# Hybrid decoder step on one core: page cache laid out for contiguous compression, keys and values multiplied page by page, more conditioning weights loaded ahead

## The chip, the core and the metric

The kernel runs on one core of a Trainium2 chip. The metric is device time of one launch in microseconds (us). TensorE (PE) multiplies, VectorE (DVE), ScalarE (ACT) and GpSimd (POOL) do the elementwise work, SyncE (SP), POOL and ACT issue transfers. Tensors lie on 128 partitions; a row of the profile such as `128x256` gives partitions by elements.

## The reference, cut to what matters

The layer is a hybrid decoder for 512 prompt tokens and 8 sample tokens of width 1024. The change touches its beginning (the conditioning, the first norm) and the compressed branch of the attention:

```python
mod = jnp.einsum("bd,de->be", jax.nn.silu(c), p["ada_w"]) + p["ada_b"]
sh1, sc1, g1, sh2, sc2, g2 = jnp.split(mod[:, None, :], 6, axis=-1)
h = _rmsnorm(x, p["norm1_w"]) * (1.0 + sc1) + sh1
proj = h @ p["w_in"]
...
def _compress(k, pe, w1, w2):          # k: (b, length, 4 heads, 64); 16 rows make a block
    sub = k[:, :nj * CMP_STRIDE].reshape(b, nj, CMP_STRIDE, N_KV_HEADS, ATT_HEAD_DIM)
    hid = jnp.einsum("ld,lde->e", pe, w1)
    for r in range(nsub):              # nsub = 2: each window is two blocks
        part = jnp.einsum("bjshd,sde->bjhe", sub, w1[r * CMP_STRIDE:(r + 1) * CMP_STRIDE])
        hid = hid + part[:, r:r + nc]
    return jnp.einsum("bnhe,ed->bnhd", jax.nn.silu(hid), w2)
...
past = cache_nsa_kv[page_table]        # 16 pages of 128 rows: k_cmp, v_cmp, k_sel, v_sel
```

For the samples `_compress` runs on the cached keys and values of 16 pages, for the prompt on those just projected. Behind it come a state-space scan, the attention, an output projection and a feed-forward block.

## The kernel before

All activations stand transposed: features on partitions, tokens in the free dimension. A dense product of one 128-wide output tile is 8 steps over k; each step is three products (high by high, high by low, low by high; the weights and the activations are split into two float32r parts) of the two halves of the tokens, six matmuls. `Weights` loads tiles ahead into a few raw buffers and splits them by half tiles: the high part on ACT (L302), the low part in turn on DVE and POOL (L304). `mm` (L379) issues nearly every matmul, `act` (L424), `tt` (L408), `stt` (L411) and `ts` (L416) nearly all elementwise work, so that groups of the profile go by tile names.

The program goes in stages; a planner lets a side stream (scan, attention) run between the steps of the main stream (dense products) at a ratio taken from an earlier pass, and a scheduler orders each engine's instructions.

- **Phase A** (`phase_a`, L644), the first 107 us. SP loads `w1k`, the first matrix of the key compression (`w`), and a few small arrays. POOL, in order, gathers the 16 pages of cached keys and values to be compressed (tiles `S` and `KS`, eight pages each; each gather is a transfer that POOL has to describe), loads the activations `xT` between them in four parts, then `w1v` and six tiles of conditioning weights (`ada`). All further loads of this phase are issued by SP as buffers come free. PE multiplies the pages by the compression matrices (`compress_s`, L1138: keys first, in groups of four pages, then values, in groups of eight, in 72 + 5 per step slices between other work). The norm follows: squares and their running sum `S` (ACT, DVE), the sums over features (`s<-ones,S`), their reciprocal root in five columns (`rstd5`), spread over the partitions by matmuls with the identity (`<-cst,rstdb`), copied into `rs`. Then four steps: two blocks of 256 conditioning columns (`ada`, L571: eight matmuls, a copy `adas`, two transposes, a reduction and an addition into `mod`), and `h(k)` (L692) for two of the eight feature blocks: x times rs, the scaling `a`, the high part on ACT, scale and shift on DVE, the low part on DVE. The dense products of the first two tiles (`misc` and `B`) take a block as it comes.
- **The scan**, to about 515 us: the rest of the input projection for the state-space branch, with the scan beside it.
- **The attention**, to about 1000 us. It begins with `cmp_tile` (L1073): the rotated keys and values of a head are copied by pairs of rows into `KP` (tile `K`, L1111), two copies on ACT and two on DVE for each of four heads. `compress_p` (L1162) multiplies `KP` by the same compression matrices, 32 matmuls of 132 columns, beside the dense products of the first head. `setup_c` puts the position table into `KP` by eight small transfers.
- Output projection and feed-forward to the end.

A float32 matmul leaves two records in the profile (and two rows of the counts there), a float32r one leaves one. The loops the steps turn on are these: the moving operand of the compression reads one element in eight.

```python
self.mm(o[:, x:x + n], w1[:, j, half, i, :], KS[x // 8][:, x % 8:x % 8 + n, j, :, i:64:8], ...)   # L1149
self.mm(pp, w[:, i * P:(i + 1) * P], self.KP[:, j, :, pr:pr + 257:8], ...)                         # L1173
```

Of the kernel before, what the change touches and what calls it, by code (L numbers as in the profile page):

```python
# [37 lines left out]
def _in_proj_tiles():  # L38
    """Column lists of w_in, one per 128-wide tile, in the order of use (-1 is a zero column)."""
# [66 lines left out]
NC0 = 72  # L106
NC1 = 5
# [29 lines left out]
def layout(a):  # L137
    """Inputs of kernel() -> arrays of the launch: layout only, and constants of the shapes."""
# [26 lines left out]
    r["pek"] = np.ascontiguousarray(a["cmp_pe_k"].reshape(16, P).T)  # L165
    r["pev"] = np.ascontiguousarray(a["cmp_pe_v"].reshape(16, P).T)
    cache = a["cache_nsa_kv"]
    ks = cache[:, :, 0:2].reshape(NPAGE, 64, 2, 2, N_KV, 64)
    r["pool_cmp"] = np.ascontiguousarray(ks.transpose(0, 2, 5, 3, 4, 1)).reshape(NPAGE * P, 512)
# [49 lines left out]
def unlayout(o):  # L219
    """Arrays of the launch -> the reference's outputs: layout only."""  # L220
# [22 lines left out]
class Weights:  # L243
    """Operand tiles in their order of use: loaded ahead, and split, half a tile at a time, into two float32r parts that
    add up to them.

    Without an order (the first of two passes) it takes them as they are asked for, and notes the order."""
# [3 lines left out]
    def __init__(self, nc, pool, jobs, order, raws=2, parts=5, queue=None):  # L251
        """queue(i): the function that issues load number i."""
        self.queue = queue
# [22 lines left out]
    def load(self):  # L276
        while self.loaded < len(self.order) and len(self.raw) < self.raws:
            i = self.loaded
            src, nk, _ = self.jobs[self.order[i]]
            pool, n = self.place(("r", i), [("r", j) for j in self.raw], self.more and self.more[1])  # L280
# [5 lines left out]
    def prepare(self):  # L286
        """Split the next half tile, if there is room for its parts."""
# [26 lines left out]
    def get(self, key):  # L314
        """The next tile: itself if it is not split, else its number for half()."""
# [17 lines left out]
    def half(self, i, x):  # L333
        """The parts of half x of tile number i."""
# [3 lines left out]
    def drop_half(self, i, x):  # L338
        """These parts are no longer read."""
# [4 lines left out]
    def drop(self, key):  # L344
        """A tile that is not split is no longer read."""
# [5 lines left out]
class Aside(float):  # L351
    """A cost in a mix of streams, but none of the stream's."""


class Emit:
# [29 lines left out]
    def after_side(self, r):  # L385
        """Keep a matmul of the main stream from running far ahead of the side stream."""
# [4 lines left out]
    def queue(self, out, src):  # L391
        """A load behind the one queued before it."""
# [7 lines left out]
    def behind(self, r, last):  # L400
        """Issue r behind the instruction last of the same engine."""
# [242 lines left out]
    def phase_a(self):  # L644
        nc, A, cp = self.nc, self.A, self.cp
        with self.tc.tile_pool(name="pa", bufs=1, reuse_waits="tile") as pa:
# [28 lines left out]
            def some(n):  # L675
                for _ in range(n):
                    next(comp, None)
# [1251 lines left out]
```

## Time and profile before

| | |
|---|---|
| time, three runs | 1514.46 us median (1514.32 to 1515.28) |
| span of the profiled execution | 1514.7 us |
| PE busy | 1450.5 us (96%) |
| DVE, ACT, POOL busy | 944.1 (62%), 696.0 (46%), 471.9 (31%) us |
| moved | 195.34 MB, mean 129 GB/s |

The span goes from the first to the last instruction of one profiled execution and stands 0.2 us from the median of the unprofiled runs. In the rows below, a line begins with its start and its duration in us or, in the grouped views, with the line of the kernel; `xN` counts instructions, and a bracket tells how long the engine had been idle and what ended that. A PE duration contains the drain of the last matmul, so the pace of a stream is read from starts.

### The profile page before, as it was taken

The page shows a single profiled execution, that of the slowest core. Times are in us where ns is not written, and L with a number is a line of the kernel's source. Part 1 is how long each engine was busy: PE and PEld are TensorE (multiplying, and loading weights), DVE is VectorE, ACT ScalarE, POOL GpSimd, SP SyncE. Part 2 cuts the span into 40 slices and gives each one's busy share as a digit, 9 for nine tenths or more (in the row PEclk, how much of TensorE's full clock was granted, in tenths as well). Part 3 has the DMA queues.
Part 4 walks back from the last instruction along what each step waited for, and adds up shares of the span by engine and source line. Part 5 has one row for each costly group of instructions (what it writes and reads, how often), then busy time and mean ns, then how long its engine had stood idle before and what let it go on. Part 6 is the DMA issues. An engine that isn't in the chain of part 4 may idle for free.

```text
span 1514.7 us, 28764 instructions
## 1 busy us (share of the span) xinstructions
PE 1450.5 (96%) x11327; PEld 1302.7 (86%) x11327; DVE 944.1 (62%) x1851; ACT 696.0 (46%) x1538; POOL 471.9 (31%) x479
## 2 busy tenths in 40 slices
PE   6989899999999899999999999999989999999996
PEld 6569789998998889787878877779989999999996
DVE  1368899879788854866768562124476635653663
ACT  1246666565565324655546463213454423432443
POOL 6112454554473745212203011112431111111113
PEclk9999999999999999999999999999999999999998
DMA  8445545446345274313122124334522234423221
GB/s 289 155 157 156 175 149 171 154 133 202 112 154 177 92 256 165 128 55 117 64 85 78 50 98 148 118 97 178 196 76 93 84 98 140 139 98 100 89 75 57
DMA packets 74807, 195.34 MB, mean 129 GB/s; under 512 B 9488, under 2 KB 22320, under 8 KB 74416
## 3 DMA queue, kind: packets, MB, share of 16 engines
q1 hardware_dynamic: 69840, 178.25, 35.7%
q0 software_dynamic: 4288, 14.72, 2.8%
q8 instruction: 89, 1.46, 0.4%
q10 hardware_dynamic: 544, 0.54, 0.1%
q14 instruction: 46, 0.38, 0.1%
HBM read 173.15 MB, written 24.49 MB: 130 GB/s over the span
## 4 chain that ended last, share of the span: by engine, by line
PE 72%; DVE 8%; DMA 3%; POOL 3%; ACT 2%; issue 2%; SPq 0%; DVEq 0%; POOLq 0%; ACTq 0%
PE d L379 54%; PE s L379 14%; PE s L1342 2%; DVE st L411 1%; DVE S L408 1%; DMA wr<-w_in 1%; DVE wl L304 1%; POOL wl L304 1%; DVE so L408 1%; DVE E L408 1%; POOL sq L408 1%; DMA st<-sst 1%; ACT so L424 1%; POOL yd L408 1%; ACT E L424 0%
## 5 line engine op out<-in xcount | busy, mean ns | idle before, releaser
L379 PE MATMUL d<-S,wh 128*128 128x256 f32 (+1 forms) x4640 | 838.9, 291 | 27.1 <-DVE S L408 9.9
L379 PEld LDWEIGHTS d<-S,wh 128*128 128x128 f32 x4640 | 673.3, 191 | 61.1 <-issue 34.0
L379 PE MATMUL d<-S,wl 128*128 128x256 f32 (+1 forms) x2672 | 559.4, 287 | 0.0
L379 PEld LDWEIGHTS d<-S,wl 128*128 128x128 f32 x2672 | 423.3, 190 | 6.9 <-issue 6.3
L304 POOL TENSOR_TENSOR wl<-wr,wh 128x512 fp32r<-128x512 f32 (+1 forms) x153 | 210.2, 1375 | 664.4 <-ACT wh L302 607.7
L302 ACT ACTIVATE wh<-wr 128x512 fp32r<-128x512 f32 (+1 forms) x354 | 217.0, 623 | 401.5 <-PE d L379 319.8
L304 DVE TENSOR_TENSOR wl<-wr,wh 128x512 fp32r<-128x512 f32 (+1 forms) x201 | 154.2, 767 | 112.4 <-ACT wh L302 99.9
L379 PE MATMUL d<-M,wh 128*128 128x256 f32 (+1 forms) x960 | 197.3, 284 | 1.5 <-DVE M L411 0.8
L379 PEld LDWEIGHTS d<-M,wh 128*128 128x128 f32 x960 | 149.8, 188 | 2.1 <-DVE M L411 1.0
L424 ACT ACTIVATE P<-s,sm 128x256 f32<-128x256 f32 (+3 forms) x128 | 66.8, 525 | 64.6 <-DVE sm L1324 60.5
L408 DVE TENSOR_TENSOR S<-S,S 128x520 f32<-128x520 f32 (+3 forms) x86 | 65.1, 760 | 34.5 <-ACT S L424 32.0
L1324 DVE TENSOR_REDUCE sm<-s 128x1 f32<-128x512 f32 (+3 forms) x96 | 57.2, 596 | 31.5 <-PE s L379 30.6
L424 ACT ACTIVATE S<-S 128x520 f32<-128x520 f32 (+4 forms) x87 | 49.7, 579 | 52.5 <-DMA S<-xT 24.3
L411 DVE SCALAR_TENSOR_TENSOR S<-d,fww,S 128x511 f32<-128x511 f32 x84 | 62.9, 749 | 12.0 <-ACT S L424 12.0
L424 ACT ACTIVATE PT<-s 128x512 f32<-128x512 f32 (+2 forms) x96 | 49.9, 524 | 38.8 <-PE s L1342 38.5
L411 DVE SCALAR_TENSOR_TENSOR st<-st,dts,so 128x128 f32<-128x128 f32 x128 | 59.7, 516 | 11.3 <-ACT so L424 7.7
L379 PE MATMUL s<-PT,V 128*64 128x128 f32 x640 | 64.3, 286 | 0.0
L379 PE MATMUL s<-K,Q 128*128 128x256 f32 (+3 forms) x256 | 60.2, 337 | 1.7 <-ACT PT L424 1.6
L416 DVE TENSOR_SCALAR P<-P,sm,gates 128x256 f32<-128x256 f32 (+3 forms) x128 | 59.7, 487 | 2.4
L424 ACT ACTIVATE so<-bcb,xd 128x128 f32<-128x128 f32 x128 | 41.0, 391 | 38.1 <-DVE ys L1033 30.5
L411 DVE SCALAR_TENSOR_TENSOR S<-d,cwh,S 128x511 f32<-128x511 f32 (+2 forms) x72 | 53.3, 741 | 1.6 <-ACT S L424 1.2
L1342 PE MATMUL s<-cst,P 128*128 128x128 f32 x320 | 52.3, 275 | 0.9 <-DVE P L416 0.7
(304 smaller groups left out, 1744.5 us busy)
## 6 DMA issues: line engine op xcount, KB each, us to landing
wr<-w_in SPq DMA_DIRECT2D x77, 512.0 KB, 3.8
wr<-w_up SPq DMA_DIRECT2D x44, 512.0 KB, 3.7
wr<-ada SPq DMA_DIRECT2D x42, 512.0 KB, 3.8
st<-sst SPq DMA_DIRECT2D x32, 256.0 KB, 2.7
csb<-dr_cs SPq DMA_DIRECT2D x16, 512.0 KB, 3.7
o_ssms<-st SPq DMA_DIRECT2D x32, 256.0 KB, 3.0
wr<-w_so SPq DMA_DIRECT2D x16, 512.0 KB, 3.7
wr<-w_dn SPq DMA_DIRECT2D x16, 512.0 KB, 3.5
```

The lines of the kernel that those rows point to most:

```text
L302: self.nc.scalar.activation(hi[:, :n], raw[:, k0:k1], AF.Copy)
L304: eng.tensor_tensor(out=lo[:, :n], in0=raw[:, k0:k1], in1=hi[:, :n], op=ALU.subtract)
L379: r = self.nc.tensor.matmul(out, lhsT=l, rhs=r, start=start, stop=stop)
L408: return (eng or self.nc.vector).tensor_tensor(out=out, in0=a, in1=b, op=op)
L411: return self.nc.vector.scalar_tensor_tensor(out=out, in0=a, scalar=s, in1=b, op0=op0, op1=op1)
L416: return (eng or self.nc.vector).tensor_scalar(out=out, in0=a, scalar1=s1, scalar2=s2, op0=op0, op1=op1)
L424: return self.nc.scalar.activation(out, a, func, scale=scale, **kw)
L1324: nc.vector.tensor_reduce(sm[:, 0], ps, AX.X, ALU.max, negate=True)
L1342: nc.tensor.transpose(ps[:, i * n + k * P:i * n + (k + 1) * P], pr[:, i, k * P:(k + 1) * P], self.ident)
```

## The change

The cached pages are laid out on the host as (8, 8) row pairs with the block position i outside: the eight rows that one matmul reads now lie side by side. `compress_s` is one nest: for each group of four pages, keys and values, both halves, eight i, so 128 matmuls of 128 columns in all where there were 64 of 128 and 32 of 256. Its sums stand in the two double-bank tiles `d`. The prompt's `KP` has the same order, so `cmp_tile` writes it contiguously from a source that is read every 16th element, and the position table comes by one transfer and two POOL copies. SP loads `w1k` and `w1v` first; POOL gathers eight pages before the first part of x. The first eight `ada` tiles get buffers of their own (`first`, in two 16 KB tiles) besides the six raw ones, and all 14 are queued on POOL at once. Twelve bf16 matmuls of zeros stand at PE's start. The table for the square root is loaded early. The sums of the norm stand before the last group of pages, the spreading behind it in two halves, and x times rs stands ahead of the `h(k)` steps.

```diff
-    r["pool_cmp"] = np.ascontiguousarray(ks.transpose(0, 2, 5, 3, 4, 1)).reshape(NPAGE * P, 512)
+    ks = cache[:, :, 0:2].reshape(NPAGE, 8, 8, 2, 2, N_KV, 64)
+    r["pool_cmp"] = np.ascontiguousarray(ks.transpose(0, 3, 6, 4, 2, 5, 1)).reshape(NPAGE * P, 512)
...
+            self.warm(pa)
...
+            for j, nm in enumerate(("w1k", "w1v")):
+                for half in range(2):
+                    self.queue(w1[:, j, half], A[nm][half])
+                if j == 0:
+                    self.queue(cT, A["cT"])
...
-                if i % 4 == 3:
-                    k = i // 4 * 2
-                    self.queue_pool(x[:, k:k + 2], A["xT"][:, k:k + 2])
-            for half in range(2):
-                self.queue_pool(w1[:, 1, half], A["w1v"][half])
+                if i in (7, 11):
+                    load_x((i - 7) // 2)
+            load_x(4)
+            load_x(6)
+            first = [self.t(cp, "S16", [P, 4, 1024], 4) for _ in range(2)]
             W = Weights(nc, pa, self.jobs(), self.order and self.order[0], raws=RAW0, parts=PART0,
-                        queue=lambda i: self.queue_pool if i < RAW0 else self.queue)
+                        queue=lambda i: self.queue_pool if i < 8 + RAW0 else self.queue,
+                        first=[first[i // 4][:, i % 4] for i in range(8)])
...
+        for x in range(0, 16, 4):
+            for j in range(2):
+                for half in range(2):
+                    for i in range(8):
+                        self.mm(ps[j][:, half, x:x + 4], w1[:, j, half, i, :],
+                                KS[x // 8][:, x % 8:x % 8 + 4, j, i].rearrange("p x (h n) -> p x h n", h=4),
+                                start=(i == 0), stop=(i == 7))
...
-            src = R[64 * j:64 * j + 64, 0:SEQ].rearrange("p (n s) -> p n s", s=2)
+            src = R[64 * j:64 * j + 64, 0:SEQ].rearrange("p (n i s) -> p i n s", i=8, s=2)
...
-                self.mm(pp, w[:, i * P:(i + 1) * P], self.KP[:, j, :, pr:pr + 257:8], start=(pr == 0), stop=(pr == 15))
+                self.mm(pp, w[:, i * P:(i + 1) * P], self.KP[:, j, i, :, half:half + 33], start=(pr == 0), stop=(pr == 15))
```

On PE at the start, in the kernel before, the keys of all pages (`s_127`, `s_128`: the two halves) stand first, then the values, cut up by the sums and the conditioning:

```order
L379 MATMUL s_127<-KS_86,w_10_81 128x4x4x8 x8
L379 MATMUL s_128<-KS_86,w_10_81 128x4x4x8 x8
L379 MATMUL s_199<-S_11_85,w_10_81 128x8x4x8 x8
L379 MATMUL s_199<-KS_86,w_10_81 128x8x4x8 x3
L379 MATMUL s_208<-ones_64,S_23_209 128x1 x5
L379 MATMUL s_259<-wr_109,sc_124 32x256 x4
L379 MATMUL s_259<-wr_111,sc_124 32x256 x4
L379 MATMUL s_199<-KS_86,w_10_81 128x8x4x8 x3
```

In the changed kernel (`d_154` keys, `d_155` values):

```order
L385 MATMUL d_154<-S_13_102,w_11_94 128x4x4x8 x16
L385 MATMUL d_155<-S_13_102,w_11_94 128x4x4x8 x16
L385 MATMUL d_154<-S_13_102,w_11_94 128x4x4x8 x16
L385 MATMUL d_155<-S_13_102,w_11_94 128x4x4x8 x16
L385 MATMUL d_154<-KS_103,w_11_94 128x4x4x8 x16
L385 MATMUL d_155<-KS_103,w_11_94 128x4x4x8 x16
L385 MATMUL s_252<-ones_64,S_24_253 128x1 x5
L385 MATMUL d_154<-KS_103,w_11_94 128x4x4x8 x16
L385 MATMUL d_155<-KS_103,w_11_94 128x4x4x8 x16
L385 MATMUL s_338<-cst_63,rstdb_291 128x128 x2
```

The whole compression now stands ahead of the conditioning; only the five sums of the norm cut into it.

On ACT behind the squares, before (`ch`: a copy of a compression's sums, `rs`: the reciprocal root on all partitions):

```order
L424 ACTIVATE ch_18_193<-s_128 128x512
L424 ACT_TABLE_LOAD
L424 ACTIVATE rstd_239<-rstd_238 128x5
L424 ACTIVATE adas_285<-s_259 128x256
L424 ACTIVATE adas_287<-s_272 128x256
L424 ACTIVATE rs_237<-d_250 128x520
```

In the changed kernel, at the same place:

```order
L430 ACTIVATE rstd_282<-rstd_281 128x5
L308 ACTIVATE wh_0_419<-wr_134 128x512
L308 ACTIVATE wh_1_444<-wr_134 128x512
L430 ACTIVATE ch_36_325<-d_154 128x512
L308 ACTIVATE wh_0_450<-wr_136 128x512
L308 ACTIVATE wh_1_492<-wr_136 128x512
L430 ACTIVATE ch_38_331<-d_155 128x512
L430 ACTIVATE rs_337<-s_338 128x256
L430 ACTIVATE rs_337<-s_342 128x264
```

The splits of the first two dense tiles (`wr_134`, `wr_136`) moved ahead of `rs`.

On POOL the transfers behind the gathers, in the changed kernel (before, `w1v` and six `ada` tiles stood there, and SP issued the first `w_in` tiles):

```order
L403 DMA S_7_87<-xT 128x1040 x2
L403 DMA S_15_124<-ada 128x1024 x4
L403 DMA S_16_125<-ada 128x1024 x4
L403 DMA wr_134<-w_in 128x1024
L403 DMA wr_136<-w_in 128x1024
L403 DMA wr_138<-ada 128x1024
L403 DMA wr_140<-ada 128x1024
```

The two `w_in` tiles moved from SP to POOL, behind eight tiles of `ada`. Behind the scan every engine's instructions stand in the order of before, apart from the shapes of the `KP` copies and the loads of the position table; within the scan the scheduler swaps neighbours on all engines.

## Rows read from the trace of the kernel before

**Rows 1.** The page: busy time of PE, share, instructions.

```profile
PE 1450.5 (96%) x11327; PEld 1302.7 (86%) x11327; DVE 944.1 (62%) x1851; ACT 696.0 (46%) x1538; POOL 471.9 (31%) x479
```

**Rows 2.** Waits of PE over the span: us in total, times, longest.

```profile
PE s L379 <- DMA S<-pool_cmp,idx: 11.9, 1, 11.9
```

**Rows 3.** Groups by shape, PE, first 100 us: busy us, mean ns.

```profile
L379 PE MATMUL s<-KS,w 128*128 128x256 f32 x32 | 16.0, 646 | 0.0
L379 PE MATMUL s<-S,w 128*128 128x256 f32 x32 | 15.6, 643 | 0.0
L379 PE MATMUL s<-S,w 128*128 128x128 f32 x64 | 15.3, 415 | 11.9 <-DMA S<-pool_cmp,idx 11.9
L379 PE MATMUL s<-KS,w 128*128 128x128 f32 x64 | 15.1, 412 | 0.0
```

**Rows 4.** Timeline of PE, stretches of phase A and of the attention's beginning.

```profile
44.68 4.78 PE L379 MATMUL s<-S,w 128*128 128x256 f32 x10
49.28 2.94 PE L379 MATMUL s<-KS,w 128*128 128x256 f32 x6
52.04 1.19 PE L379 MATMUL s<-ones,S 128*128 128x1 f32 x10
...
61.13 1.28 PE L379 MATMUL d<-cst,rstdb 128*128 128x128 f32 x10
...
105.14 0.40 PE L379 MATMUL d<-S,wl 128*128 128x256 f32 x2
...
552.38 3.52 PE L379 MATMUL s<-K,wr 128*128 128x132 f32 x14
559.07 1.21 PE L379 MATMUL d<-S,wh 128*128 128x256 f32 x4 [3.17 <-DVE S L408]
...
577.56 1.02 PE L379 MATMUL s<-PT,sTn 128*128 128x512 f32 x2
578.01 1.04 PE L379 MATMUL d<-S,wh 128*128 128x256 f32 x4
```

**Rows 5.** Timeline of ACT: the last two squares of the norm.

```profile
32.17 1.16 ACT L424 ACTIVATE S<-S 128x520 f32<-128x520 f32 x2 [5.16 <-DMA S<-xT]
```

**Rows 6.** Transfers of the first 50 us: GB/s in 40 slices of 1.25 us.

```profile
GB/s 0 18 156 400 364 295 256 197 287 385 282 239 230 312 333 259 190 257 366 315 243 203 342 366 361 325 400 419 419 419 419 331 59 10 0 192 18 0 0 0
```

**Rows 7.** Timeline of DVE: a step h(k) of phase A, the last one's end, the copies.

```profile
63.05 0.19 DVE L408 TENSOR_TENSOR mod<-mod,cst 128x32 f32<-128x32 f32 x1
63.16 1.91 DVE L408 TENSOR_TENSOR S<-S,rs 128x520 f32<-128x520 f32 x3
64.99 0.25 DVE L411 SCALAR_TENSOR_TENSOR a<-mod,cst 128x16 f32<-128x16 f32 x2
68.21 0.23 DVE L408 TENSOR_TENSOR S<-S,a 128x8 f32<-128x8 f32 x2
68.37 0.99 DVE L416 TENSOR_SCALAR S<-S,a,mod 128x512 f32<-128x512 f32 x2
71.13 0.68 DVE L304 TENSOR_TENSOR wl<-wr,wh 128x512 fp32r<-128x512 f32 x1
...
100.62 1.30 DVE L408 TENSOR_TENSOR S<-S,S 128x520 fp32r<-128x520 f32 x2
```

**Rows 8.** Timeline of ACT: `rs`, and a tile's splits.

```profile
62.45 0.60 ACT L424 ACTIVATE rs<-d 128x520 f32<-128x520 f32 x1 [0.80 <-PE d L379]
...
67.78 2.18 ACT L302 ACTIVATE wh<-wr 128x512 fp32r<-128x512 f32 x4
```

**Rows 9.** Windows: length; busy of PE, PEld, DVE, ACT, POOL; clock; DMA; GB/s.

```profile
12.00:42.00 30.00, 30.00 (x129) 27.19 (x130) 4.91 (x7) 4.65 (x8) 16.36 (x22) 1.00 0.85 302
...
520.00:530.00 10.00, 7.59 (x57) 7.54 (x56) 9.46 (x13) 4.27 (x10) 7.40 (x10) 0.90 0.50 149
```

**Rows 10.** All instructions on tile `K` by duration (ns min/median/max).

```profile
L379 PE MATMUL s<-K,wr x64: 396/419/462, 546.1 to 592.3; 128*128 128x132 f32 x64
L1088 DVE COPY K<-S x8: 287/289/1551, 523.2 to 535.7; 64x256 f32<-64x256 f32 x8
```

More of the change, by code (lines that the diff above doesn't have):

```diff
@@ L105 @@
 PART0 = 4
-NC0 = 72
-NC1 = 5
+WARM = 12
 F_CHUNKS = [(0, 8), (8, 8), (16, 6)]
@@ L249, with __init__ @@
     HALF = 4
-    def __init__(self, nc, pool, jobs, order, raws=2, parts=5, queue=None):
-        self.queue = queue
+    def __init__(self, nc, pool, jobs, order, raws=2, parts=5, queue=None, first=()):
+        self.queue, self.first = queue, list(first)
         self.nc, self.pool, self.jobs, self.raws, self.parts = nc, pool, jobs, raws, parts
@@ L276, in load @@
     def load(self):
-        while self.loaded < len(self.order) and len(self.raw) < self.raws:
-            i = self.loaded
+        while self.loaded < len(self.order):
+            i, m = self.loaded, len(self.first)
             src, nk, _ = self.jobs[self.order[i]]
+            if i < m:
+                self.queue(i)(self.first[i][:, :nk * P], src)
+                self.raw[i] = self.first[i]
+                self.loaded += 1
+                continue
+            if sum(j >= m for j in self.raw) >= self.raws:
+                break
             pool, n = self.place(("r", i), [("r", j) for j in self.raw], self.more and self.more[1])
@@ L351 @@
 class Aside(float):
+    pass
 class Emit:
@@ L642, in preload, with warm @@
         self.tc.keep_in_program_order(self.act(self.t(self.cp, "tbl", [P, 1]), self.eps, func))
+    def warm(self, pool):
+        z = self.t(pool, "warm", [P, 512], dt=BF16)
+        self.nc.gpsimd.memset(z, 0.0)
+        d = self.ps_s()
+        for _ in range(WARM):
+            self.mm(d, z[:, 0:P], z)
     def phase_a(self):
@@ L672, in phase_a @@
             self.ts(self.sc, tn, 0.5)
+            self.preload(AF.Sqrt)
             comp = self.compress_s(KS, w1, pa)
-            def some(n):
-                for _ in range(n):
-                    next(comp, None)
-            some(NC0)
+            for _ in range(3):
+                next(comp)
             d = self.ps_s()
@@ L686, in phase_a @@
             self.sums(d, sq, True, True)
+            rb = self.rstd5(d, DM, pa)
+            for _ in comp:
+                pass
             r = self.t(pa, "rs", [P, T])
-            self.act(r, self.rstd(d, DM, pa))
+            for part in range(2):
+                lo, hi = self.span(part)
+                cs = self.PARTS[part]
+                self.act(r[:, lo:hi], self.spread(rb[:, cs[0]:cs[-1] + 1], part))
             self.h_hi = self.t(cp, "S16", [P, KD, T], 4, F32R)
             self.h_lo = self.t(cp, "S16", [P, KD, T], 4, F32R)
+            for k in range(2):
+                self.tt(x[:, k, :], x[:, k, :], r, ALU.mult)
             def h(k):
@@ L718, in phase_a @@
                     h(2 * nb + 1)
-                some(NC1)
+                    if nb < 3:
+                        for k in (2 * nb + 2, 2 * nb + 3):
+                            self.tt(x[:, k, :], x[:, k, :], r, ALU.mult)
             for n, g in zip(names, tiles):
@@ L724, in phase_a @@
                     self.early[n] = e.value
-            some(999)
             self.setup_const()
@@ L1081, in cmp_tile @@
         for j in range(2):
[L1082 removed]
+            src = R[64 * j:64 * j + 64, 0:SEQ].rearrange("p (n i s) -> p i n s", i=8, s=2)
             for s in range(2):
[L1084 removed]
+                dst = self.KP[64 * s:64 * s + 64, j, :, h, 0:32]
                 if s == j:
[L1086 removed]
+                    self.act(dst, src[:, :, :, s])
                 else:
[L1088 removed]
+                    nc.vector.tensor_copy(dst, src[:, :, :, s])
         self.done.add(("cmp", h))
@@ L1110, in setup_c @@
         self.vn = self.t(pc, "vn", [NB, 2, 4, 64])
-        self.KP = self.t(pc, "K", [P, 2, 4, 272], 2)
-        for j, nm in enumerate(("pek", "pev")):
-            for h in range(4):
-                nc.sync.dma_start(self.KP[:, j, h, 256:272], A[nm])
+        self.KP = self.t(pc, "K", [P, 2, 8, 4, 34], 2)
+        pe = self.t(pc, "SC", [P, 2, 8, 2], 1)
+        nc.sync.dma_start(pe, A["pe"])
+        for j in range(2):
+            nc.gpsimd.tensor_copy(self.KP[:, j, :, :, 32:34], self.bc(pe[:, j], 2, 4))
         for j in range(2):
```

42 lines of the change are left out of this document (15 added, 27 removed).

## The prediction

> **What bounds the kernel now.** The page first: PE is busy 96% of the span [rows 1], so what counts is PE's work and PE's waits. Its waits by releaser have one long entry, 11.9 us until the first pages land [rows 2]. In phase A, up to the first dense product that is not fed by h(k) (the last one fed by it starts at 105.14 and ends about 105.5 [rows 4]), PE looks full as well, but the groups by shape say with what: the compression, s<-S,w and s<-KS,w, is 62.0 us of the first 100 in four rows [rows 3]. The pace of these matmuls is out of line. Ten of 256 columns take 49.28 - 44.68 = 4.60 us [rows 4], 0.46 us each or 1.80 ns a column; 64 of 128 columns take 15.3 us [rows 3], 0.238 each or 1.86 ns a column; the prompt's, of 132 columns, take about 0.24 (14 in 3.52 less a drain of 0.2 [rows 4]), 1.8 ns a column. Two float32 records of 512 columns read in order take 578.01 - 577.56 = 0.45 us [rows 4], 0.44 ns a column. The three slow kinds share the moving operand that takes every eighth float. The third writes its sums contiguously, the first two in runs of eight, and all have the same price: it is the reading. So phase A is bound by strided reads, not by arithmetic and not by the gathers, which PE no longer waits for after 11.9.
>
> **The change part by part.** *Compression of the pages.* 256 records of 128 columns in place of 128 of 128 and 64 of 256. Streaming would be 128 x 0.44 = 56 ns; the weights of each have to be loaded too, and streams of little else run at 1.19 / 10 = 0.119 (sums) and 1.28 / 10 = 0.128 (spreading) [rows 4]. I take 0.12: 30.7 us. Bounds are 0.056 (the streaming alone) and 0.24 (no gain); 0.12 is taken because these two rows load weights of the same 128 by 128 float32.
>
> [...] By rows: a copy of 256 elements takes 0.287 us on DVE [rows 10]; at the slow reads' 1.8 ns an element it would be 0.46 plus its fixed part, so 0.2 us more, 8 copies on each engine, where DVE is 9.46 of 10 us busy and PE waits [rows 9]. I charge 1 us (0 to 4, the upper end if a copy slowed fourfold as the matmuls did and half of it reached PE).
>
> *When it can start and end.* `w1v` (1.05 MB) now comes before the first group, on SP, so I put PE's start at 13 instead of 11.9. The gathers keep their pace of four pages in some 5.3 us, less than the 7.7 us that PE takes for a group (64 x 0.12), so PE sets the end: 13 + 30.7 + 1.2 for the sums = 44.9. The last part of x is squared from 32.17 on [rows 5]; with 1 MB more in front I take 33.5, and the sums are wanted at 13 + 3 x 7.7 = 36.1: no wait. Spreading adds 1.3 [rows 4]: 46.2.
>
> *Loads.* The slices show 419 GB/s while the old `ada` loads ran, empty after about 40.3 us [rows 6]. By then the same bytes are moved in the new kernel (w1v is only earlier). Four more tiles of 0.52 MB come before both `w_in` tiles are in: 2.1 MB / 419 GB/s = 5.0, landed at 45.3. This matters because ACT, which works in order, has the splits of these two tiles ahead of `rs`, so `rs`, then every h(k), and PE behind them, stand behind a load. Two splits of the second tile 1.1 (4 in 2.18), the copy `ch` 0.6, `rs` in two halves about 0.7 [rows 8]: `rs` ends at 45.3 + 2.4 = 47.7, and not at 46.2 + 0.7.
>
> *The chain of h(k).* From there DVE sets the pace, as its order shows. Eight x times rs at 1.91 / 3 = 0.64: 5.1, to 52.8. Then for the first four blocks: `chs` 0.9, four reductions and additions in `mod` at about 0.5 (0.19 for an addition, 0.3 for a reduction), four `a` at 0.13, eight narrow ones at 0.12, four scalings at 0.5, four low parts at 0.65 [rows 7]: 0.9 + 2.0 + 0.5 + 1.0 + 2.0 + 2.6 = 9.0, to 61.8. For the next two: 0.5 + 0.25 + 0.5 + 1.0 + 1.3, and three weight splits of 0.68 [rows 7] that stand among them: 5.6, to 67.4. The last two: 1.0 + 0.25 + 0.5 + 1.0 + 1.3 = 4.1, to 71.5. Handing over between ACT and DVE in each of three steps adds some 2: 73.5. Before, the last low part ended at 100.62 + 1.30 = 101.92 [rows 7]. The dense products behind it are the same, so phase A is 101.92 - 73.5 = 28.4 us shorter; I take 28. The later `ada` tiles need no wait any more, PE has the conditioning done by about 54.
>
> *The prompt's compression.* 64 records [rows 10] from 0.24 to 0.12. Fourteen of them run just before PE idles 3.17 us for DVE at 559.07 [rows 4], and their gain only lengthens that wait; the other 50 are worth 6.0. There the weight tiles land just in time, so I take 5 (2 to 7).
>
> *At nothing.* Twelve matmuls of zeros stand where PE idles 11.9 us [rows 2]; in the window behind, the granted clock is 1.00 without them [rows 9], so they also win nothing. The early root table and the one transfer for the position table are off the path: seven issues fewer on SP ahead of loads that wait for buffers anyway. The scan's swaps of neighbours: 0, with 3 either way.
>
> **Sum**: 1514.7 - 28 - 5 + 1 = 1482.7 against the profiled span, 0.2 less against the median: **1482**.
>
> **The rivals.** *A. The forecast.* 1482.
>
> *B. Loads instead of PE.* Fourteen `ada` and `w_in` tiles queue behind x, with SP's loads beside them. While gathers mix in, the mean was 302 GB/s [rows 9]. If the ten tiles that `rs` now waits for move at that rate, they take 5.24 / 0.302 = 17.4 us instead of 12.5, `rs` is 5 us late and all behind it: 1487. For it: the splits ahead of `rs` on ACT. Against it: 419 GB/s in the slices right after the gathers [rows 6]. If x also comes some us later, 1490.
>
> *C. PE ahead of DVE.* If the scheduler's DVE chain hands over without the 2 us and starts 3 us sooner (the two tiles in by 42.3), the last low part moves from 73.5 to 68.5, and the prompt gives its 7: 1475.5, called 1475.
>
> *D. The writes.* The sums of the pages are written in runs of eight floats, before and after. If these set the 0.238, the nest costs 256 x 0.238 = 60.9 us, PE leaves it at 75.1, and with the same 28.6 us from there (73.5 - 44.9) the last low part ends at 103.7, 1.8 later than before; only the prompt's compression, written in order, gains: 1514.5 + 1.8 - 5 + 1 = 1512. Against it: the prompt's reads were as slow with contiguous writes. [...]
>
> *E. Slower.* The pace belongs to the pair of a float32 weight load and its matmul, whatever it reads. Then 256 x 0.24 = 61.4 replaces 62.0, PE leaves the nest at 13 + 61.4 + 1.2 = 75.6, and the last low part ends 2.3 us later than before; the prompt gains nothing, and the copies cost their 1 to 4: 1518 to 1521. It decides from 0.24 a record on. Against it stand the sums and the spreading, which load weights of this size at 0.12 to 0.13.
>
> **How the numbers follow.** Chances: A 0.66, B 0.16, C 0.11, D 0.04, E 0.03. The range takes A with its bounds (phase A 24 to 32, the prompt 2 to 7, the copies 0 to 4, the scan 3), B and C: 1474 to 1491; D and E stay out. A measurement of this kernel tells about 0.2%, 3 us, from no change. Faster by more: A, B, C and half of D, 0.95; within: the rest of D and the edge of E, 0.03; slower 0.02.
>
> **What would show it.** In the changed trace: records of d<-S,w and d<-KS,w 0.12 us apart, back to back from about 13 to 45 (0.24 would be D or E, gaps between groups would put the gathers in front); ACT idle before wh of the first tile, until about 44 to 46, and `rs` at 47 to 48 (over 52: B); the last S<-S,S of phase A at 73 or so; s<-K,wr at 0.12; copies into K of 0.3 to 0.5 us. Wrong would be the forecast if the clock stayed low in the nest, if the gathers set its pace, or if the time saved came back as waits in the scan.

## The result, and the profile after

The changed kernel takes 1492.22 us (median of four runs, 1486.78 to 1494.21) against 1514.74: 0.9846 of the time before (95% interval 0.983 to 0.9862). That is 1.5% faster, by 22 us where 32 were forecast, and 1.2 us beyond the slow end of the range. Its runs lie 7 us apart, those of before 1 us. The profiled run is one of its slower ones (1494.21, span 1492.4).

The page's first line and PE's timeline of phase A (start, duration, engine, line, operands, shape, count; in brackets the idle time before and what ended it):

```profile
PE 1424.6 (95%) x11403; PEld 1294.2 (87%) x11403; DVE 940.5 (63%) x1851; ACT 697.5 (47%) x1540; POOL 473.9 (32%) x488
```

```profile
1.39 5.28 PE L385 MATMUL s<-warm 128*128 128x512 bf16 x12 [1.39 <-POOL warm L653]
13.24 9.06 PE L385 MATMUL d<-S,w 128*128 128x128 f32 x64 [6.57 <-DMA S<-pool_cmp,idx]
23.07 1.00 PE L385 MATMUL d<-S,w 128*128 128x128 f32 x5 [0.77 <-DMA KS<-pool_cmp,idx]
24.51 0.71 PE L385 MATMUL d<-S,w 128*128 128x128 f32 x4 [0.43 <-issue]
25.94 0.50 PE L385 MATMUL d<-S,w 128*128 128x128 f32 x3 [0.73 <-issue]
27.37 7.41 PE L385 MATMUL d<-S,w 128*128 128x128 f32 x52 [0.92 <-issue]
34.61 7.31 PE L385 MATMUL d<-KS,w 128*128 128x128 f32 x64
41.76 1.17 PE L385 MATMUL s<-ones,S 128*128 128x1 f32 x10
42.79 7.39 PE L385 MATMUL d<-KS,w 128*128 128x128 f32 x64
50.02 1.18 PE L385 MATMUL s<-cst,rstdb 128*128 128x128 f32 x10
```

The four rows of 62.0 us [rows 3] are gone: in the third group 64 records take 7.15 us from start to start (34.61 to 41.76), 0.112 each, and in the fourth the same. But the nest ends at 50.0, not at 44.9: the first group takes 9.06, and the second comes in pieces until 27.37 (the first pause, 0.77, is put down to a page of `KS`, which this group does not read). The windows (length; busy time and count of PE, PEld, DVE, ACT, POOL; granted clock; DMA share; GB/s) tell the two apart:

```profile
13.20:17.00 3.80, 3.76 (x18) 3.79 (x19) 0.00 (x0) 0.00 (x0) 2.89 (x5) 0.53 0.79 228
17.00:22.30 5.30, 5.30 (x48) 5.11 (x46) 0.70 (x1) 1.16 (x2) 4.35 (x5) 1.00 0.86 282
22.30:27.30 5.00, 2.10 (x13) 1.90 (x13) 1.40 (x2) 1.16 (x2) 4.12 (x6) 0.97 0.84 280
27.30:30.30 3.00, 2.93 (x14) 2.91 (x14) 0.00 (x0) 0.00 (x0) 3.00 (x6) 0.50 0.92 340
```

At 0.112 the first window would hold 34 records, not 18 (1.8 us lost at a granted 0.53, records 0.213 apart), the third 45, not 13 (3.6 us, at a granted 0.97: a stall), the fourth 27, not 14 (1.5 us, at a granted 0.50 behind the stall). ACT and DVE from there on, the rows that answer to [rows 7, 8]:

```profile
43.72 1.15 ACT L308 ACTIVATE wh<-wr 128x512 fp32r<-128x512 f32 x2 [0.34 <-DMA wr<-w_in]
46.65 0.60 ACT L430 ACTIVATE ch<-d 128x512 f32<-128x512 f32 x1 [1.78 <-PE d L385]
47.14 1.14 ACT L308 ACTIVATE wh<-wr 128x512 fp32r<-128x512 f32 x2
50.27 0.60 ACT L430 ACTIVATE ch<-d 128x512 f32<-128x512 f32 x1 [1.99 <-PE d L385]
50.76 0.86 ACT L430 ACTIVATE rs<-s 128x256 f32<-128x256 f32 x2
```

```profile
51.66 4.97 DVE L414 TENSOR_TENSOR S<-S,rs 128x520 f32<-128x520 f32 x8 [3.03 <-ACT rs L430]
62.03 2.53 DVE L414 TENSOR_TENSOR S<-S,S 128x520 fp32r<-128x520 f32 x4
68.05 3.50 DVE L414 TENSOR_TENSOR S<-S,S 128x520 fp32r<-128x520 f32 x2
73.38 0.69 DVE L310 TENSOR_TENSOR wl<-wr,wh 128x512 fp32r<-128x512 f32 x1 [1.23 <-ACT wh L308]
77.18 1.30 DVE L414 TENSOR_TENSOR S<-S,S 128x520 fp32r<-128x520 f32 x2
```

The early weight tile was there at 43.7; what `rs` waited for is PE. Phase A ends at 78.5 instead of 101.9. Behind it about 4 us come back: PE's first dense product after `Z` starts 23.4 us earlier than before, the first transpose of the scan 20.8, and from 152 us on it is 19.3. In the trace before, and after:

```profile
107.19 0.75 PE L379 MATMUL d<-S,wh 128*128 128x256 f32 x4 [1.66 <-ACT Z L424]
132.99 0.27 PE L894 MATMUL s<-cst,X 128*128 128x128 f32 x1
```

```profile
83.77 0.74 PE L385 MATMUL d<-S,wh 128*128 128x256 f32 x4 [1.66 <-ACT Z L430]
84.95 1.16 PE L385 MATMUL d<-S,wh 128*128 128x256 f32 x4
105.97 0.71 PE L385 MATMUL d<-S,wh 128*128 128x256 f32 x4 [1.13 <-DVE S L417]
112.16 0.27 PE L921 MATMUL s<-cst,X 128*128 128x128 f32 x1
```

In the attention, tile `K` answers to [rows 10]: the matmuls are as forecast (a piece of 14 takes 1.74 us, where it took 3.52), the copies dearer.

```profile
L385 PE MATMUL s<-K,wr x64: 273/276/428, 530.0 to 571.1; 128*128 128x132 f32 x64
L1115 DVE COPY K<-S x8: 368/491/2446, 503.9 to 517.3; 64x256 f32<-64x256 f32 x8
```

### The profile page after: what moved, and what is told of

Read it like the earlier page. It is cut to its first block, busy times and chain, and to the rows that moved or that the text cites. A ratio compares the mean times of both kernels' runs of the same rounds, so it can differ in the third digit from the quotient of the medians.

```text
span 1492.4 us, 28896 instructions
## 1 busy us (share of the span) xinstructions
PE 1424.6 (95%) x11403; PEld 1294.2 (87%) x11403; DVE 940.5 (63%) x1851; ACT 697.5 (47%) x1540; POOL 473.9 (32%) x488
## 4 chain that ended last, share of the span: by engine, by line
PE 75%; DVE 9%; DMA 6%; issue 3%; ACT 3%; POOL 3%; SPq 0%; DVEq 0%; ACTq 0%; POOLq 0%
PE d L385 57%; PE s L385 14%; PE s L1370 2%; DMA wr<-w_in 2%; DVE st L417 1%; DMA csx<-dr_cs 1%; DVE S L414 1%; DVE E L414 1%; POOL wl L310 1%; DVE wl L310 1%; ACT wh L308 1%; ACT S L430 1%; DMA csb<-dr_cs 1%; DMA P<-pool_kv,idx 1%; ACT E L430 1%
## 5 line engine op out<-in xcount | busy, mean ns | idle before, releaser
L310 POOL TENSOR_TENSOR wl<-wr,wh 128x512 fp32r<-128x512 f32 (+1 forms) x153 | 206.7, 1352 | 624.0 <-ACT wh L308 568.8
L430 ACT ACTIVATE S<-S 128x520 f32<-128x520 f32 (+4 forms) x87 | 49.6, 580 | 51.0 <-DVE S L414 20.9
L417 DVE SCALAR_TENSOR_TENSOR st<-st,dts,so 128x128 f32<-128x128 f32 x128 | 55.6, 483 | 5.5 <-ACT so L430 4.7
```

The source lines that it names most:

```text
L310: eng.tensor_tensor(out=lo[:, :n], in0=raw[:, k0:k1], in1=hi[:, :n], op=ALU.subtract)
L417: return self.nc.vector.scalar_tensor_tensor(out=out, in0=a, scalar=s, in1=b, op0=op0, op1=op1)
L430: return self.nc.scalar.activation(out, a, func, scale=scale, **kw)
```

## Experiments

Each run is given by its median time and by its ratio to the kernel before on the same chip, with the ratio's 95% interval. Unless said otherwise an edit starts from the changed kernel.

### The changed kernel again

> The changed kernel once more, for the scatter of its time (1486.8 to 1494.2 where the kernel before stays within 1 us). If the scatter is made at the start, the profiled execution shows another length of the stall in the second group of pages (5 us in the first profile) or another clock there, and the stretches from 140 us on are the same within 1 us. If it is made later, the first 80 us agree and a later stretch differs.

1489.4 us, 0.9844 (0.9821 to 0.9866). The stall is there again, and now begins inside the first group, after 57 records, whose four pages had all been waited for at its first record; so it is no wait for pages:

```profile
12.70 8.34 PE L385 MATMUL d<-S,w 128*128 128x128 f32 x57 [6.23 <-DMA S<-pool_cmp,idx]
21.43 0.69 PE L385 MATMUL d<-S,w 128*128 128x128 f32 x4 [0.40 <-issue]
22.86 0.60 PE L385 MATMUL d<-S,w 128*128 128x128 f32 x4 [0.74 <-issue]
...
27.19 7.95 PE L385 MATMUL d<-S,w 128*128 128x128 f32 x57 [0.42 <-issue]
```

The scatter is not made at the start. This profile is 2.3 us behind the first one from 84 us on and 5.7 us ahead of it from 550 us on: 4 come in the scan and 4 at the prompt's compression, where the first profile waited for a late weight tile:

```profile
558.97 0.80 PE L385 MATMUL s<-K,wr 128*128 128x132 f32 x4 [2.67 <-DMA wr<-w1v]
```

(from the first profile; here the longest such wait is 0.78).

### Which part brings the time

The new nest with the old layout of the pages:

```diff
-    r["pool_cmp"] = np.ascontiguousarray(ks.transpose(0, 3, 6, 4, 2, 5, 1)).reshape(NPAGE * P, 512)
+    r["pool_cmp"] = np.ascontiguousarray(ks.transpose(0, 2, 5, 3, 4, 1)).reshape(NPAGE * P, 512)
...
-    KS[x // 8][:, x % 8:x % 8 + 4, j, i].rearrange("p x (h n) -> p x h n", h=4),
+    KS[x // 8][:, x % 8:x % 8 + 4, j, :, i:64:8],
```

> The changed kernel with the pages laid out as before, so that the nest's matmuls read every eighth float again (order, writes, loads as in the changed kernel). If the reads set the pace: 256 records 0.24 us apart, the nest ends at about 75 instead of 50.0, and the time is about 1492 + 25 = 1517. If the order, the writes or the weight loads did it: records stay at 0.11 and the time at 1492.

1514.17 us, 1.001 (0.9998 to 1.0021). The same records in the same order, with the same writes, take 0.234 again (12.70 to 42.71 for 128), and the whole gain is gone, although the new prompt's side is still in:

```profile
12.70 30.19 PE L385 MATMUL d<-S,w 128*128 128x128 f32 x128 [6.37 <-DMA S<-pool_cmp,idx]
42.71 13.48 PE L385 MATMUL d<-KS,w 128*128 128x128 f32 x57
```

The other way round, the kernel before with the contiguous layout of the pages and nothing else (the host's layout, the shape of the tiles and the operand that `compress_s` reads):

> The kernel before with one part of the change alone: pages laid out for contiguous reading, the order (keys by four pages, values by eight, slices between the norm and the conditioning), loads and the prompt's side as before. By the pace of the changed kernel (0.88 ns a column) its 128 records of 128 and 64 of 256 columns take 28.4 us instead of 62.0. If the reads carry the gain of phase A: the last low part at about 80 instead of 101.9, time 1492 to 1495. If order and loading ahead carry half of it: it ends at about 90, time 1502 to 1505.

1490.49 us, 0.9852 (0.9831 to 0.9873): as fast as the whole change. The last low part of phase A even ends earlier, at 77.2. Here PE does wait for pages, twice and whole, with no pieces:

```profile
23.21 3.81 PE L379 MATMUL s<-KS,w 128*128 128x128 f32 x32 [2.34 <-DMA KS<-pool_cmp,idx]
29.07 5.43 PE L379 MATMUL s<-KS,w 128*128 128x128 f32 x32 [2.05 <-DMA KS<-pool_cmp,idx]
```

The kernel before with the prompt's side alone (`KP`, its copies, the position table):

```diff
-                self.mm(pp, w[:, i * P:(i + 1) * P], self.KP[:, j, :, pr:pr + 257:8], start=(pr == 0), stop=(pr == 15))
+                self.mm(pp, w[:, i * P:(i + 1) * P], self.KP[:, j, i, :, half:half + 33], start=(pr == 0), stop=(pr == 15))
```

> The kernel before with the prompt's side alone (KP in the order of the matmuls, copies from every 16th element, position table in one transfer). The prediction gave 5 for the matmuls and took 1 for the copies: 1514.5 - 4 = 1510.5. If the copies cost what they gain: 1514.5 within 1.5; s<-K,wr at 0.12 a record and DVE's copies at 0.37 to 0.5 us in either case.

1509.45 us, 0.9974 (0.9964 to 0.9985): 3.9 us, as the terms of the prediction have it. The opposite edit, the prompt's side undone in the changed kernel, was too fine for that kernel's scatter:

> The changed kernel with the prompt's side undone (KP, its copies and its position table as in the kernel before, matmuls reading every eighth float). By the two traces the new prompt's side is worth 4.3 us at its matmuls' end and costs 2 to 3 at its copies, so undoing it should cost about 2: 1491, with 16 copies back at 0.29 (DVE) and 0.42 us (ACT), and s<-K,wr back at 0.24 a record. By the prediction's terms (5 gained, 1 paid) it would cost 4: 1493.

1492.74 us, 0.986 (0.9839 to 0.9881), against 0.9844 and 0.9846 with it: 2 us for the new side, within the interval of none and of 4.

Both layouts in the kernel before, and nothing else:

> The kernel before with both layouts read contiguously (pages and the prompt's side) and nothing else of the change: order, loads, no zeros as before. If the two gains measured alone add up (22.4 and 3.9), 1514 - 26 = 1487 to 1488, 1 to 3 below the changed kernel, whose other parts then cost these. If the stages hide one another's gain, 1490, as with the pages alone.

1486.86 us, 0.9826 (0.9806 to 0.9846). The two gains add up, and the rest of the change (order by pages, loads ahead, zeros) shows no gain beside them; by the medians it rather costs 3 us, but the intervals overlap. Of that rest, loading ahead is good. Without the tiles `first`:

```diff
-                        queue=lambda i: self.queue_pool if i < 8 + RAW0 else self.queue,
-                        first=[first[i // 4][:, i % 4] for i in range(8)])
+                        queue=lambda i: self.queue_pool if i < RAW0 else self.queue)
```

> The changed kernel without the eight tiles of conditioning weights in buffers of their own: six tiles ahead, as in the kernel before. If loading ahead carries a part of phase A, the conditioning of the steps 2 to 4 waits for loads and the time grows by 3 to 8 (1493 to 1497). If DVE's chain is the slower one anyway, it stays at 1489 to 1490; below it, if the early loads stand in the way of pages and weights that are needed sooner.

1493.97 us, 0.9877 (0.9861 to 0.9893), some 5 us slower: PE waits for `ada` tiles at 55 and 61 us (1.01 and 0.98).

### The zeros and the clock

```diff
-            self.warm(pa)
```

> The changed kernel without its twelve matmuls of zeros. In the changed kernel the first 64 records of the nest take 9.1 us (the others 7.3), at a granted clock of 0.63 in their first 5 us, and the second 64 stall three times between 22.3 and 27.4. Theory 'PE runs out of instruction code' (an instruction transfer lands at 26 to 27): 24 PE instructions fewer ahead of the nest, so the stall comes about 12 records later or is shorter. Theory 'pages land late': the stall stays at the same time, 22.3 to 27.4. On the clock: if the zeros keep it up, the first 64 take over 9.1 us and the time grows by 1 to 3; if their end, an idle stretch after a busy one, is what lowers it, the first 64 take 7.3 us as nothing was lowered in the kernel before, and the time falls by up to 2.

1487.42 us, 0.9826 (0.9805 to 0.9847): 2 us faster without the zeros by the medians, with overlapping intervals, and the nest ends 2.5 earlier (47.84 for 50.38 in the repeated run). The stall is as before (65 records, then pieces from 22.62 until 26.93), not 12 records later. With 26 zeros instead of 12:

> The changed kernel with 26 matmuls of zeros instead of 12, so that they last until just before the first pages (12 took 5.3 us, 26 take some 11). If an idle stretch after the zeros lowers the clock: the first 64 records at 0.112, 7.2 us instead of 9.1, about 2 us faster. Theory 'code': 28 more PE instructions ahead of the nest, so the stall comes some 14 records earlier, inside the first group of pages, or its code arrives early enough to be gone. Theory 'pages': the stall stays at 22.3 to 27.4 us.

1490.37 us, 0.9847 (0.9827 to 0.9866); the first 68 records take 10.8 us, the clock stays at 0.50 until 18. The 26 zeros take 7.31 us and not 11, so PE still idles 4.0 us before the first pages (6.2 to 6.6 with twelve), and the guess on an idle stretch behind the zeros is not tested. Theory 'code' fails here too: the stall comes after 68 records, not 14 earlier than with twelve zeros (57 to 66). Nor do the 16 KB transfers of instructions fit: one starts at 26.45 in the first profile, at 32.06 in the repeated one, 5 us behind the end of its stall. Windows of the run without zeros:

```profile
12.70:16.00 3.30, 3.30 (x16) 3.30 (x17) 0.00 (x0) 0.00 (x0) 2.69 (x4) 1.00 0.72 214
17.00:21.00 4.00, 4.00 (x38) 4.00 (x37) 0.70 (x1) 1.17 (x2) 3.09 (x5) 1.00 0.80 269
```

The granted clock reads 1.00, and yet the records of the first window start 0.213 apart until 15.79, as those of the changed kernel do at 0.50, and 0.112 apart from there on. The trace of this run has no entry of the clock before 15.76, where one of 1.00 begins, and the view counts a stretch without an entry as 1.00; so the row does not show that the clock was high, and the pace is the one that the changed kernel had at a granted 0.50. Without zeros the nest starts as slowly; from the end of the stall to its own end it takes 20.9 us, 23.2 in the repeated run, so what it is spared is the second low stretch.

### What the stall hangs on

Plain transfers of fixed pages in place of the gathers (another content):

```diff
-                g = self.gather(KS[i // 8][:, i % 8].rearrange("p j i c -> p (j i c)"), A["pool_cmp"], i)
+                g = nc.gpsimd.dma_start(KS[i // 8][:, i % 8].rearrange("p j i c -> p (j i c)"), A["pool_cmp"][P * i:P * (i + 1)])
```

> The changed kernel with plain transfers of fixed pages in place of the sixteen gathers (the page table is left out, so the cached pages are other ones; bytes, tiles and queue are the same, and POOL describes a transfer in about 0.6 us instead of 1.25). Theory 'gathers': PE stalls in the second 64 records because something that the gathers occupy feeds it, so without gathers the 256 records run in one piece at 0.112, 29 us from the first page on, and the nest ends at 41 to 43 instead of 50. Theory 'PE's own supply': whatever feeds the pages, after 57 to 68 records at this pace PE stalls for some 5 us.

1483.52 us, 0.9794 (0.9777 to 0.9812), no stall, spreading from 43.84. Here the first pages come 1.2 to 1.7 us earlier. To see that it is not the earlier pages, each page's number is read into a register and the page fetched by a plain transfer, still on POOL and no faster than before:

```diff
+                v = nc.gpsimd.value_load(self.pg[0:1, i:i + 1], min_val=0, max_val=NPAGE - 1)
+                self.queue_pool(KS[i // 8][:, i % 8].rearrange("p j i c -> p (j i c)"), A["pool_cmp"][bass.ds(v * P, P)])
```

> The changed kernel, whole, with each page number read into a register and the page fetched by a plain transfer at that address, all still on POOL and in the same order, in place of the sixteen gathers. Theory 'gathers starve PE': as with fixed pages, no stall in the nest; if POOL's register reads are cheap, the nest ends at 44 to 46 and the time is about 1484 to 1486. Theory 'the gain of the fixed pages was their earlier arrival only': the page number is waited for again, pages come later, the stall is back and the time is 1489.

1488.92 us, 0.9822 (0.9802 to 0.9842). Again no stall, though the last page is issued at 24.6 and the transfers move 270 GB/s between 20 and 27 us as in the changed kernel (268). The nest ends at 45.1, 5 us earlier than in the first profile, and yet the time misses the expected 1484 to 1486: the last low part of phase A ends at 77.6 (78.5 and 80.3 in the two profiles of the change), because ACT now waits for the early weight tile until 44.24, and `rs` behind it. All loads on SP instead (`nc.sync`, `self.queue`):

> The same with pages, activations and all early weight tiles issued by SP in one line, in the order pages 0 to 7, x, pages 8 to 11, x, pages 12 to 15, x, weights. Against the run on POOL it shows who issues best. If SP's register reads cost little, as above or 1 to 2 us better (1482 to 1486); if each read and issue holds SP for over 1.5 us, pages come at the gathers' pace or slower and the nest ends at 48 or later.

1486.12 us, 0.9815 (0.9797 to 0.9832), again without a stall. Now sixteen small gathers on POOL beside pages that come by SP:

```diff
+                g = self.gather(dm[:, i], A["pool_cmp"].rearrange("r (a b) -> (r a) b", b=8), i)
```

> Pages by register and SP as above, x and weights on POOL as in the changed kernel, and on POOL, where the gathers stood, sixteen gathers of 32 bytes a partition that nobody reads (extra work). Theory 'the describing of gathers on POOL starves PE': though all pages land early, PE stalls in pieces of 1.4 us with some four records each until the last of these gathers is described, about 26 us. Theory 'late pages' or 'bytes': no stall, since the pages are there and 65 KB in all are added.

1487.96 us, 0.9829 (0.981 to 0.9848), and no stall; the theory that POOL's describing starves PE falls. POOL describes one at 22.01, where the changed kernel stalls, and PE goes on through all 128 records of the first two groups:

```profile
22.01 1.34 POOL L1168 DMA_INDIRECT dm<-pool_cmp,idx  x1 [0.30 <-issue]
```

```profile
12.99 17.00 PE L385 MATMUL d<-S,w 128*128 128x128 f32 x128 [7.31 <-DMA S<-pool_cmp]
```

At last whole gathers that PE does not read (the first eight into `first`, the others into the unread `KS`):

> Sixteen whole gathers on POOL as in the changed kernel, but PE reads none of them: pages 0 to 7 come to it by plain transfers of SP at a register's address, and the third and fourth group of the nest read these pages again (pages 8 to 15 are left out of the compression, so that its sums are other ones). From about 20 us on PE has all that it reads. Theory 'gathers with their data slow PE': pieces of 1.4 us with three to six records each, up to 27 us, as in the changed kernel. Theory 'the stall belongs to what PE reads': no pieces, 11 to 12 records a us from 18 us on, as in the runs with page numbers in registers.

1494.05 us, 0.9869 (0.9854 to 0.9884). A shorter stall is back, after 66 records, ending at 27.05, at a granted 1.00 from 22 to 32 us:

```profile
15.82 9.34 PE L385 MATMUL d<-S,w 128*128 128x128 f32 x66 [9.81 <-DMA S<-pool_cmp]
25.61 0.48 PE L385 MATMUL d<-S,w 128*128 128x128 f32 x2 [0.45 <-issue]
26.32 0.27 PE L385 MATMUL d<-S,w 128*128 128x128 f32 x1 [0.23 <-issue]
27.05 13.98 PE L385 MATMUL d<-S,w 128*128 128x128 f32 x123 [0.46 <-issue]
```

So in these runs the stall shows only with whole gathers in flight and a PE that takes records at 0.112. It begins after 57 to 68 records in all seven profiles that have it and ends at 26.9 to 27.4, whenever it began. These two conditions do not always bring it: in the run with the pages' layout alone PE takes the 32 records from 23.21 on in one piece, at 0.112, while the last two gathers are described (23.95 to 26.15). What PE lacks meanwhile stays open: not the pages, not the granted clock, not the transfers' bandwidth, not POOL's time, and not its code by the signs above.

### Other sizes, and a faster version

Eight pages to a matmul, the sums behind the nest:

```diff
-        for x in range(0, 16, 4):
+        for x in range(0, 16, 8):
```

> The changed kernel with eight pages to a matmul (256 columns, half as many records), the sums of the norm behind the second group. If a record of 128 columns lasts as long as its weight load, one of 256 columns lasts about as long (256 x 0.44 ns = 0.113 us), so the nest takes 2 x 7.3 us behind pages 8 and 16 and ends at 38 instead of 50. But in its ACT order the reciprocal root now stands behind the splits of both early weight tiles, which land at 43.7 and about 46.5. If these loads bound it, rs ends at 50 to 51 as in the changed kernel (51.6) and the time stays at 1489 (within 2); if PE's nest is all that bounds it, rs ends at 43 and the time falls by 8.

1494.36 us, 0.9856 (0.983 to 0.9881). The price was wrong: a record of 256 columns takes (47.90 - 34.09) / 64 = 0.216 us from start to start, twice that of 128, so the columns set it and not the weight load, and the nest ends at 47.9. It starts at 17.28, when eight pages are there; there is no stall, but until 23.1 the granted clock is 0.50 and a record takes 0.427:

```profile
34.09 13.98 PE L385 MATMUL d<-KS,w 128*128 128x256 f32 x64
```

The same, the splits of the early weight tiles held behind `rs`, no zeros:

> As the run with eight pages to a matmul, and the splits of the early weight tiles behind rs in ACT's order, and no matmuls of zeros. Nest ends at 38, sums 39.2, rs at 43 to 44 instead of 51.6. DVE then has x times rs done at 49 instead of 56.6; the conditioning copies wait on ACT for the two weight tiles until 47 to 49. Last low part of phase A at 71 to 73 instead of 78.5: time about 1489 - 6 = 1483 if the scan keeps it, 1487 if the scan's start gives part of it back again.

1495.43 us, 0.9868 (0.9848 to 0.9889). A miss: with the nest at 47.5 there was nothing to win ahead of `rs`, and DVE's eight products took 7.13 us instead of 4.97.

Pages by number on SP, no zeros:

> The changed kernel with pages by number on SP (1486.1 in its run) and without the matmuls of zeros, which alone were worth 2 us (1487.4 against 1489.4). If the half-clocked first 5 us of the nest come from the zeros, the first 64 records now take 7.3 us and the time is 1484. If PE starts at half its pace after any idle stretch, as the run without zeros suggests (6 to 7 records in each of the first 4 us), the first 64 take 8.5 to 9 and the time stays within 1 of 1486.

1484.53 us, 0.981 (0.9795 to 0.9825): the fastest whole kernel here, 30 us below the kernel before, by its median 5 below the change. The first 64 records take 8.96 us (8.5 to 9 was expected if the slow start does not come from the zeros), while the time is the 1484 of the other guess:

```profile
12.73 16.27 PE L385 MATMUL d<-S,w 128*128 128x128 f32 x128 [12.73 <-DMA S<-pool_cmp]
28.84 7.31 PE L385 MATMUL d<-KS,w 128*128 128x128 f32 x64
35.99 1.17 PE L385 MATMUL s<-ones,S 128*128 128x1 f32 x10
```

With no stall ACT waits for the early weight tile, and `rs` ends at 47.4, as the prediction had it (47.7):

```profile
42.99 1.15 ACT L308 ACTIVATE wh<-wr 128x512 fp32r<-128x512 f32 x2 [5.38 <-DMA wr<-w_in]
46.71 0.66 ACT L430 ACTIVATE rs<-s 128x256 f32<-128x256 f32 x2
```

The same with the root spread inside the last group and the splits behind `rs`:

> The run with pages by number on SP and without zeros (1484.5), with the reciprocal root spread between the two halves of the last group and ahead of the early weight splits in ACT's order. If the nest, through rs and DVE's eight products, still sets the end of phase A: rs at 42 instead of 47.4, products done at 48 instead of 52.4, the last low part 2 to 4 us earlier than 75.4, time 1481 to 1483. If the conditioning (ready at 52 to 54) or the weight splits are as late as these, nothing moves: 1484 to 1485.

1489.63 us, 0.9832 (0.9813 to 0.985), not faster. `rs` ends at 44.8 instead of 47.4, but the products now run beside POOL's low parts of the splits and end at 52.0, where they did anyway (52.4); the last low part ends at 77.2, 1.8 us later:

```profile
44.86 7.15 DVE L417 TENSOR_TENSOR S<-S,rs 128x520 f32<-128x520 f32 x8 [1.40 <-ACT rs L433]
```

## Why the prediction was right, and where it was wrong

**The bound: right.** Strided reading set the price; writes and weight loads did not (1.001 where it was put back, 0.9852 where it alone was taken away; 0.234 us a record against 0.112 with the same writes and weights). Rivals D and E are out: the nest writes in runs of eight and runs at 0.112, no slower than the spreading (0.111 from start to start), which writes in order.

**The pace: right in size, for a wrong reason.** 0.12 was taken from the weight loads, with 0.44 ns a column for the streaming. That row was misread: the group behind the two records of 512 columns starts at 578.01, but takes 1.04 us for four records [rows 4], where such a group elsewhere takes 0.64, because the second record still runs: it starts at 577.99 and takes 0.59. By the 0.40 us that the group loses, the two take 0.85 us, 0.83 ns a column, and by this estimate 128 columns make 0.11 by streaming alone. Eight pages to a matmul showed it: 0.216 us for 256 columns. (The 0.238 of the old pace holds drains; from start to start it is 0.236.) The two records that one float32 matmul leaves here take 0.84 to 0.87 ns a column each.

**When the nest ends: the step that failed.** "PE sets the end: 13 + 30.7 + 1.2 = 44.9" supposed that PE, once started, is fed. At 0.112 it would have been 13.2 + 28.6 + 1.0 = 42.9; the slow start took 1.8, the stall and the low clock behind it 5.3: 50.0. What it leaned on, "the gathers keep their pace", is true, and the pages were no wait; the gathers hurt otherwise, and only at the new pace; how is open. With plain transfers of fixed pages phase A ends at 73.0, forecast 73.5, and the time is 0.9794, 1483 of 1514.5 us; that this meets the forecast is partly luck, since there the pages come 1.2 to 1.7 us earlier and the weight tile at 38.2 instead of 45.3. With plain transfers by page number it is 1484.5 to 1489.6.

**The whole sum.** In the profiled run 32 us were forecast against the span and 22.3 came: 23.4 for 28 in phase A, 4.1 given back in the scan where nothing was, 2.1 for 4 on the prompt's side, and 0.9 more behind it. The three signs that the prediction itself named as wrong all showed in part: a low clock in the nest, the gathers in its way, time given back in the scan. The repeat's median, 1489.4, lies inside the range; that is the scatter of the same kernel, and the failed step is the same in both.

**What sets `rs`: wrong for the change.** The last load ahead of it was to land at 45.3; ACT's last two splits began at 47.14, behind a copy that waited for PE. Rival B's sign, `rs` near 52, came by another cause. Without the stall the load did set it, and `rs` ended at 47.4 to 48.6 in the four runs by page number whose ACT order was kept.

**DVE's chain: right.** From `rs` to the last low part 26.9 us, forecast 25.8; in it are the pair at 68.05, 3.50 where 1.30 was counted (two subtractions of POOL, 2.99 us, run beside it), and the split that waits at 73.38; other parts were quicker.

**The scan: 0 within 3** was forecast; 4 came back in the first profile, 1.6 of it at a low clock from 84.95 on (0.53 granted until 86.11, four records in 1.16 instead of 0.64), 1.6 in two waits for DVE (1.13 at 105.97, 0.43 at 113.19).

**The prompt's side: right.** 5 less 1, and 3.9 measured alone; in the two profiles of the change it is 2 and 6, by the chance of one weight tile. The copies, with medians of 0.38 to 0.49 us for 0.29, are dearer by 0.1 to 0.2 us, where 0.2 was estimated from the matmuls' 1.8 ns; they read every 16th float where they read every 2nd, but they also write in runs of 32 floats now, where they wrote in order, and no run takes the two apart.

**"At nothing": wrong for the zeros**, which cost some 2 us by the medians: they did lie in idle time, but the clock was low a second time behind the stall (0.50 from 27.3 to 30.3). And the 1.00 of the window behind [rows 9] does not show the nest's start: in that trace, too, the clock has no entry before 15.99.

## What to carry to other kernels

Price a matmul by the stride of its moving operand before its shape (here 1.8 ns a column at every eighth float, 0.84 to 0.87 in order): here the layout of one array carried all that a rewritten stage brought, and a run of each part alone would have said so first. Where a consumer becomes twice as fast, every supply that was hidden at the old pace has to be shown again, by a stretch of the trace that runs at the new pace. In a timeline of grouped matmuls, check a price against the duration of the group behind it.

## What the runs showed of the hardware

- Whole gathers in flight slowed a PE that did not wait for them, in seven profiles: 13 records in 5 us instead of 45 in the first. Plain transfers of the same bytes did not (270 GB/s between 20 and 27 us in the run by page number on POOL, 268 in the changed kernel). In two runs whose PE had just waited for pages, 32 records passed beside gathers in one piece.
- A float32 record took 0.84 to 0.87 ns a column read contiguously (0.216 us for 256 columns, 0.112 for 128) at a granted 1.00, 1.8 at every eighth float (0.234 for 128).
- In these runs strided reads did not feel the clock, contiguous ones did: records of every eighth float started 0.233 us apart at a granted 0.50 and at 0.99 (the windows also count records that only overlap them), contiguous ones of 256 columns 0.427 at 0.50 and 0.216 at 1.00.

```profile
12.70:16.00 3.30, 3.30 (x14) 3.30 (x15) 0.00 (x0) 0.00 (x0) 2.69 (x4) 0.50 0.67 221
16.00:20.00 4.00, 4.00 (x19) 3.60 (x18) 0.52 (x1) 1.16 (x2) 3.08 (x5) 0.99 0.91 304
```

(windows of the run with the old page layout)

- In the first 3 to 6 us of the contiguous nest PE worked at half its pace (0.213 us a record, then 0.112), with and without the twelve zeros. The granted 1.00 that the view gives at the start of two traces was a stretch without an entry of the clock (none before 15.76 in the run without zeros, none before 15.99 in the kernel before).
- DVE's eight products of 520 columns took 4.97 us alone and 7.15 with two subtractions of POOL (3.06 us) beside them.
